# Where a kernel squares its input for the first RMS norm: transposed tiles in the first chunk, or a second, token-major load in the second chunk

## The chip, the cores and the metric

One core of one Trainium2 chip runs the kernel in one launch. The metric is the device time of the launch in microseconds (us); the kernel before takes 1688.6 us (median of three runs, 1688.39 to 1688.74). The five engines are named as in the profile: PE (TensorE, matmuls; PEld its weight loads), DVE (VectorE), ACT (ScalarE), POOL (GpSimd) and SP (SyncE, which here only issues transfers).

## The reference

One decoder layer for 256 tokens of width 4096, in float32: an RMS norm, one wide input projection, two attention mixers, a gate path, an output projection, a residual and a last RMS norm.

```python
h = _rmsnorm(x, norm_g[l])
proj = h @ w_in[l]
(q_a, k_a, v_a, z_a, q_b, kc, vc, ksl, vsl, kwn, vwn, z_b, g_b) = jnp.split(proj, ...)
o_a = _dilated_mixture(q_a, k_a, v_a, ...)      # dilated sliding-window attention, 16 heads
o_b = _nsa(q_b, kc, vc, ksl, vsl, kwn, vwn, ...)  # compressed, selected and window branch, 16 heads
y_a = _rmsnorm(o_a, out_g_a[l]) * silu(z_a)
y_b = _rmsnorm(o_b, out_g_b[l]) * silu(z_b)
x = x + concat(y_a, y_b) @ w_out[l]
return _rmsnorm(x, final_g)
```

The norm is `x * rsqrt(mean(x * x) + 1e-6) * g`. Its factor per token can be applied after the projection, since it is the same for all features of a token. So the sum of squares of a token isn't needed before the first product is scaled.

## The kernel before

**Tiles.** All wide products run as one stream of *chunks* of up to 512 output columns. A chunk sums over 32 *k-tiles* of 128 features, for two halves of 128 tokens. Its weights arrive in *units* of four k-tiles (1 MB) into three stage buffers. Every float32 operand is split in two float32r halves, `h` (a copy on ACT, line 102, or 105 with a scale) and `l` (the rest, on DVE, line 103 or 106), and each product is three matmuls (`mm3`, lines 95 to 97). So one k-tile costs six matmuls of 512 columns and a chunk 192. A unit is split in two half-units of two k-tiles (`split_unit`); the split runs two half-units ahead of the matmuls, in three buffers. For the first eight units, the ones of the first chunk, `split_x` also splits the k-tiles of `x`, scaled with `norm_g`, out of a transposed copy of `x` that `load_x` brings in eight pieces of 0.5 MB (SP's queue). Those pieces live in four buffers, tag `o`.

**The squares.** After the second half of each of the first eight units, `square_x` squares the piece of `x` on ACT (line 163) and POOL adds it to the squares before (line 165). When the first chunk has ended, `done_kvc` calls `token_rms`: two DVE adds (lines 176 and 177), four PE records that sum over partitions (line 180), and `rsqrt_mean` (DVE, then POOL's power, line 112). Only then ACT evicts the first chunk's two accumulators, scaled (line 513), to a tile of the tag `qk`, which has two buffers. There are four accumulators, so the third chunk needs those of the first.

**Background work.** What mixers and gates need is queued as tasks in a first-in, first-out queue. `run_stream` takes one step of it every second k-tile. The first chunk holds keys and values that are to be compressed: two `compress` tasks of 14 steps each, with their own weights (4 MB each, in the buffers of tag `o`). Chunks two to four are queries, keys and values of mixer A's first head group, whose task is queued at the end of the fourth. `hooks` calls a function at a given chunk and k-tile.

**Order.** The framework that builds the kernel orders each engine's instructions by the order of writing and by its own estimate of times, so neighbours can change places. Every engine and each transfer queue then works strictly in its order.

**The two ends.** The kernel begins with thirteen matmuls on zeros and one activation, written ahead of all loads (lines 121 to 127), to have PE and ACT's table ready. Then `run_stream` asks for three units of `x` (SP's queue) and weights (the first unit on ACT's queue, four transfers of one k-tile each, line 216). At the end the last chunk is multiplied for the first 128 tokens and then, from splits kept on chip, for the second 128; `finish` scales the residual rows of one half in eight pieces of 512 columns, in turn on DVE (line 846) and ACT (line 844), and stores each piece (line 847).

Of the kernel before, what the change touches and what calls it, by code (L numbers as in the profile page):

```python
# [11 lines left out]
F32 = mybir.dt.float32  # L12
# [33 lines left out]
# The three dilated patterns of mixer A share their scores and their ALiBi distances, so their  # L46
# softmaxes merged by their denominators are one softmax in which a key counts once for each
# pattern that holds it (MULT). With SEQ = 256 there are 4 selection blocks and SLC_TOP = 16, so
# the selected branch of mixer B holds every causal key, and its window of 512 does too.
# The columns of mixer B's scores are [window keys, later half first | compressed | selected keys].  # L50
# [28 lines left out]
def hybrid_trunk(ctx: ExitStack, tc: tile.TileContext, a: dict):  # L79
# [19 lines left out]
    def split_to(h, l, src, scale=None):  # L99
        """h + l = src * scale, both in float32r."""  # L100
        if scale is None:
            nc.scalar.activation(h, src, AF.Copy)  # L102
            nc.vector.tensor_sub(l, src, h.bitcast(F32))  # L103
        else:
            nc.scalar.activation(h, src, AF.Copy, scale=scale)  # L105
            nc.vector.scalar_tensor_tensor(l, src, scale, h.bitcast(F32), op0=OP.mult, op1=OP.subtract)  # L106

    def rsqrt_mean(out, ss, width):
        """out = (ss / width + eps) ** -0.5, for [P, n] sums of squares."""
        t = work.tile(list(out.shape), F32, name="rsq")  # L110
        nc.vector.tensor_scalar(t, ss, 1.0 / width, EPS, op0=OP.mult, op1=OP.add)
        nc.gpsimd.tensor_tensor(out, t, nhalf[:, : out.shape[1]], op=OP.pow)

# [6 lines left out]
    # while the first loads run: the tensor engine to its full clock, ScalarE's table  # L120
    idle = work.tile([P, CW], BF16, name="idle", tag="zt", bufs=4)
    nc.vector.memset(idle, 0.0)
    warm = psm.tile([P, CW], F32, name="warm", tag="ps")
    for _ in range(WARM):
        nc.tensor.matmul(warm, idle[:, :P], idle, start=True, stop=True)
    first = work.tile([P, 1], F32, name="first", bufs=1)
    nc.scalar.activation(first, ones, AF.Exp)

# [10 lines left out]
    squares = []  # L139

    x_raw = {}

    def load_x(piece):
        q, half = divmod(piece, 2)
        if half == 0:
            xh.append(big.tile([P, QK, SEQ], F32R, name=f"xh{q}", tag="x", bufs=8))
            xl.append(big.tile([P, QK, SEQ], F32R, name=f"xl{q}", tag="x", bufs=8))
        t = x_raw[piece] = big.tile([P, G4, SEQ], F32, name="xp", tag="o", bufs=4)
        step = 1 if piece == 0 else 2 if piece == 1 else G4
        for j in range(0, G4, step):  # L150
            nc.sync.dma_start(t[:, j : j + step], a["xT"][piece, :, j : j + step])
            if piece == 0 and j == 0:
                nc.sync.dma_start(g_in, a["norm_g"])

    def split_x(k):
        """One k-tile of x, times norm_g, split."""
        (q, i), (piece, j) = divmod(k, QK), divmod(k, G4)
        split_to(xh[q][:, i], xl[q][:, i], x_raw[piece][:, j], g_in[:, k : k + 1])

    def square_x(piece):  # L160
        """The squares of four k-tiles of x, added to those before."""
        sq = work.tile([P, G4, SEQ], F32, name="sq", tag="qk", bufs=2)
        nc.scalar.activation(sq, x_raw.pop(piece), AF.Square)  # L163
        if squares:
            nc.gpsimd.tensor_tensor(squares[0], squares[0], sq, op=OP.add)  # L165
        else:
            squares.append(sq)

    # 1 / rms of the tokens, and what the projections are scaled by
# [4 lines left out]
    def token_rms():  # L174
        sq = squares[0]
        nc.vector.tensor_add(sq[:, 0:2], sq[:, 0:2], sq[:, 2:4])
        nc.vector.tensor_add(sq[:, 0], sq[:, 0], sq[:, 1])
        s = psm.tile([P, NT], F32, name="ss", tag="ps")
        for m in range(NT):
            nc.tensor.matmul(s[:, m : m + 1], sq[:, 0, m * P : (m + 1) * P], ones, start=True, stop=True)  # L180
        rsqrt_mean(rstd, s, DM)
        nc.vector.tensor_scalar_mul(nrstd, rstd, -1.0)
        nc.vector.tensor_scalar_mul(rstd_q, rstd, SCALE)

# [14 lines left out]
    # A unit is one load: k-tiles k0 ... of one chunk of output columns, used in two halves.  # L199
# [11 lines left out]
    def stage_unit(u):  # L211
        src, width, k0, n, c = units[u]
        t = stage.tile([P, n, width], F32, name="w", tag="w")
        if u == 0:
            for j in range(n):
                nc.scalar.dma_start(t[:, j : j + 1], src[:, j : j + 1])
        elif u < 4:
            for j in range(0, n, 2):
                nc.sync.dma_start(t[:, j : j + 2], src[:, j : j + 2])
        else:  # L220
            nc.sync.dma_start(t, src)
        staged[u] = t

    def split_unit(u, half):
        t = staged[u]
        src, width, k0, n, c = units[u]
        n //= 2
        h = split.tile([P, n, width], F32R, name="wh", tag="wh")
        l = split.tile([P, n, width], F32R, name="wl", tag="wl")
        w = 1 if u == 0 else n  # L230
        for j in range(0, n, w):
            if u < 8:
                for k in range(k0 + half * n + j, k0 + half * n + j + w):
                    split_x(k)
            split_to(h[:, j : j + w], l[:, j : j + w], t[:, half * n + j : half * n + j + w])
        if half == 1 and u < 8:
            square_x(u)
        splitted[u, half] = (h, l)
# [4 lines left out]
    def split_held(u, half, i):  # L243
        """One eighth of the last chunk, split and kept on chip."""
# [15 lines left out]
    hooks = {}  # (chunk, k-tile): work that becomes possible there  # L260

    def run_stream():
# [4 lines left out]
        for i, (u, s) in enumerate(subs):  # L267
            while True:
                if n_st < len(units) and n_st <= u + (2 if i else 0):
                    if n_st < 8:  # L270
                        load_x(n_st)
                    stage_unit(n_st)
                    n_st += 1
                    if n_st == 6:
                        late_loads()
# [40 lines left out]
        # the last chunk again, for the second half of the tokens  # L316
# [25 lines left out]
    def evict_split(key):  # L342
        def done(ps):
            # [tokens, head, (h, l), d]: the two halves of a head side by side
# [7 lines left out]
    def transposed(src, key, tag):  # L352
        """[tokens, 4 heads * d] -> float32r halves of [d, 4 heads, tokens]."""
# [28 lines left out]
    def pipeline(units, stages, at):  # L382
        """Stage i of a unit is done at[i] steps of the background work after its first."""
# [7 lines left out]
    def attend_a(hg):  # L391
# [34 lines left out]
        def values(j):  # L426
            ph, pl, rden = live.pop(j)
            head = hg * 4 + j
            # columns: with h and with l of the values
# [55 lines left out]
    def turn_y(which, f0):  # L485
        """Features f0 * 128 ... of y (two heads), turned and split for the output projection."""
# [19 lines left out]
    # rows 0 ...: h, rows 32 ...: l, rows 64 ...: h of the compressed values, zeros between  # L506
# [10 lines left out]
    def compress(t, which):  # L517
        """gelu((blocks + pe) @ w1) @ w2 of the keys (0) or the values (1), both groups."""
# [63 lines left out]
        # gelu in its tanh form  # L582
# [39 lines left out]
    # keys and values of the two other branches: selected (0) and window (1)  # L622
# [56 lines left out]
    def attend_half(hg, m):  # L679
        """Four heads of mixer B that share their keys, one half of the tokens."""  # L680
# [52 lines left out]
        # (columns of n, halves of the values)  # L733
# [5 lines left out]
        def turn(i):  # L739
# [10 lines left out]
            if vl is None:  # L750
                # rows that meet h, l and h of the values: h, h and l
# [78 lines left out]
    def finish(m, gf):  # L830
# [4 lines left out]
        for i in range(8):  # L835
# [11 lines left out]
            nc.sync.dma_start(a["out"][m * P : (m + 1) * P, i * CW : (i + 1) * CW], t)  # L847

# [10 lines left out]
    add_chunk(w_chunk(20), CW, x_lhs, done_kvc)  # L859
# [13 lines left out]
    # y of mixer A and the first half of mixer B are turned as the last chunk frees x  # L873
# [17 lines left out]
def _tiles(w, n):  # L891
    """[4096, n * 512] -> [n, 8, 128, 4, 512]: contiguous blocks of four k-tiles."""
# [41 lines left out]
```

## Time and profile before

| What | Value |
|---|---|
| time, median of three runs | 1688.6 us (1688.39 to 1688.74) |
| profiled execution | span 1686.2 us from the first to the last instruction; its time outside the span is not given |
| PE busy | 1667.2 us (99%), 8071 matmuls |
| DVE busy | 1023.2 us (61%) |
| ACT busy | 814.7 us (48%) |
| POOL busy | 24.3 us (1%), 16 instructions |
| transfers | 319.97 MB, mean 190 GB/s over the span |
| mean granted clock of PE | 0.998 |

A row of the timeline has the start, the duration, the engine and line, the operation with the tile it writes and the tiles it reads, the number of merged instructions and, in brackets, the idle time before them with what ended it. A row of the windows table has a stretch, its length, the busy time and the number of instructions of each engine, the granted clock, the share of the transfer engines and their GB/s. A row of waits has who waited for whom, the total, the number of waits and the longest one. A row of the chain has the start, the duration and what the end of the run depended on at that time. A row of a group has its line, engine and form, the count, busy time and mean duration in ns, and the idle time ahead of it. "L96" is line 96 of the kernel; a helper's line stands for all who call it. Matmuls overlap, so a matmul's 0.39 us is longer than the distance to the next one.

### The profile page before, as it was taken

How to read it: one execution, taken by the hardware profiler on the slowest of the kernel's cores; microseconds unless marked ns; L12 is line 12 of the kernel's file. 1: busy time of each engine (PE TensorE's matmuls, PEld its weight loads, DVE VectorE, ACT ScalarE, POOL GpSimd, SP SyncE). 2: the span in 40 equal slices, each digit the busy share in tenths (PEclk: the TensorE clock that was granted, in tenths of full speed). 3: DMA queues.
4: the chain of work that ended last, by engine and by line, in shares of the span. 5: the costliest groups of instructions: out<-in, count | busy, mean ns of one | idle time of the engine just before them, and what ended most of it. 6: DMA issues, size and time to landing. Idle time of an engine off the chain costs nothing.

```text
span 1686.2 us, 20334 instructions
## 1 busy us (share of the span) xinstructions
PE 1667.2 (99%) x8071; PEld 1394.2 (83%) x8071; DVE 1023.2 (61%) x1389; ACT 814.7 (48%) x1121; POOL 24.3 (1%) x16
## 2 busy tenths in 40 slices
PE   8999999999999999999999999999999999999997
PEld 5788888888888888998888888888888888888887
DVE  8865474465456447456858678576667855555553
ACT  7654454445445445445545455454445544444443
POOL 3100000000000000000000000000000000000000
PEclk9999999999999999999999999999999999999999
DMA  8764545544554554465354444645555456655654
GB/s 321 281 250 150 199 150 191 187 171 175 199 181 169 187 190 166 139 225 186 135 190 150 175 166 146 213 151 187 193 185 196 167 202 218 213 205 212 209 199 160
DMA packets 51791, 319.97 MB, mean 190 GB/s; under 512 B 6128, under 2 KB 7664, under 8 KB 15856
## 3 DMA queue, kind: packets, MB, share of 16 engines
q1 hardware_dynamic: 47376, 311.33, 51.4%
q10 hardware_dynamic: 4320, 7.34, 1.3%
q8 instruction: 63, 1.03, 0.3%
q14 instruction: 32, 0.26, 0.0%
HBM read 314.46 MB, written 4.19 MB: 189 GB/s over the span
## 4 chain that ended last, share of the span: by engine, by line
PE 95%; DVE 2%; issue 1%; ACT 1%; DMA 1%; SPq 0%; ACTq 0%; POOLq 0%; POOL 0%; DVEq 0%
PE acc L96 29%; PE acc L95 29%; PE acc L97 29%; DVE xl L106 1%; PE pt L747 1%; DVE wl L103 1%; PE pt L361 1%; PE s L96 1%; PE s L95 1%; PE s L97 1%; ACT wh L102 0%; PE ph L572 0%; PE ph L573 0%; PE pt L496 0%; DMA w<-in_w_in 0%
## 5 line engine op out<-in xcount | busy, mean ns | idle before, releaser
L103 DVE TENSOR_TENSOR wl<-w,wh 128x1024 fp32r<-128x1024 f32 (+2 forms) x562 | 677.7, 1206 | 582.3 <-ACT wh L102 579.1
L102 ACT ACTIVATE wh<-w 128x1024 fp32r<-128x1024 f32 (+2 forms) x562 | 588.2, 1047 | 722.8 <-PE acc L97 678.4
L96 PE MATMUL acc<-wl,xh 128*128 128x512 f32 (+2 forms) x1792 | 688.0, 384 | 5.6 <-DVE wl L103 5.6
L95 PE MATMUL acc<-wh,xh 128*128 128x512 f32 (+2 forms) x1792 | 690.6, 386 | 1.6 <-ACT wh L102 1.6
L97 PE MATMUL acc<-wh,xl 128*128 128x512 f32 (+2 forms) x1792 | 686.9, 383 | 0.0
L96 PEld LDWEIGHTS acc<-wl,xh 128*128 128x128 f32 x1792 | 337.1, 188 | 71.0 <-DVE wl L103 10.0
L97 PEld LDWEIGHTS acc<-wh,xl 128*128 128x128 f32 x1792 | 336.8, 188 | 65.9
L95 PEld LDWEIGHTS acc<-wh,xh 128*128 128x128 f32 x1792 | 336.8, 188 | 64.3 <-ACT wh L102 2.5
L95 PE MATMUL acc<-wh,yh 128*128 128x512 f32 (+1 forms) x512 | 192.9, 377 | 0.0
L97 PE MATMUL acc<-wh,yl 128*128 128x512 f32 (+1 forms) x512 | 192.5, 376 | 0.0
L96 PE MATMUL acc<-wl,yh 128*128 128x512 f32 (+1 forms) x512 | 192.4, 376 | 0.0
L97 PEld LDWEIGHTS acc<-wh,yl 128*128 128x128 f32 x512 | 96.4, 188 | 17.7
L96 PEld LDWEIGHTS acc<-wl,yh 128*128 128x128 f32 x512 | 96.4, 188 | 17.5
L95 PEld LDWEIGHTS acc<-wh,yh 128*128 128x128 f32 x512 | 96.4, 188 | 17.2
L477 DVE RECIPROCAL ez<-ez 128x512 f32<-128x512 f32 x16 | 53.6, 3349 | 0.2
L704 ACT ACTIVATE nb<-nb,mn 128x128 f32<-128x128 f32 (+1 forms) x64 | 28.7, 449 | 25.8 <-DVE mn L702 24.7
L106 DVE SCALAR_TENSOR_TENSOR xl<-xp,g_in,xh 128x256 fp32r<-128x256 f32 x32 | 29.0, 943 | 5.6 <-ACT xh L105 5.6
L412 ACT ACTIVATE n<-n,mn 128x128 f32<-128x128 f32 (+1 forms) x32 | 13.4, 456 | 24.5 <-DVE mn L410 24.5
L697 DVE SCALAR_TENSOR_TENSOR nb<-cmat,s 128x272 f32<-128x272 f32 (+1 forms) x48 | 19.6, 428 | 5.9 <-PE s L97 5.7
L165 POOL TENSOR_TENSOR sq<-sq 128x1024 f32<-128x1024 f32 x7 | 20.9, 2984 | 30.5 <-ACT sq L163 30.5
L105 ACT ACTIVATE yh<-pt,g_out 128x256 fp32r<-128x256 f32 x32 | 14.5, 464 | 12.9 <-DVE yl L106 12.9
L821 DVE TENSOR_TENSOR r<-acc,xr 128x512 f32<-128x512 f32 (+1 forms) x18 | 10.6, 625 | 15.5 <-PE acc L97 15.5
(236 smaller groups left out, 957.0 us busy)
## 6 DMA issues: line engine op xcount, KB each, us to landing
w<-in_w_in SPq DMA_DIRECT2D x204, 1024.0 KB, 4.8
w<-in_w_out SPq DMA_DIRECT2D x64, 1024.0 KB, 4.8
w<-in_w_vg SPq DMA_DIRECT2D x8, 608.0 KB, 3.8
w<-in_cmp_k_w SPq DMA_DIRECT2D x4, 1024.0 KB, 8.2
w<-in_cmp_v_w SPq DMA_DIRECT2D x4, 1024.0 KB, 7.8
w<-in_w_kw SPq DMA_DIRECT2D x4, 1024.0 KB, 4.8
out<-r SPq DMA_DIRECT2D x16, 256.0 KB, 2.8
xr<-in_x ACTq DMA_DIRECT2D x7, 512.0 KB, 5.2
```

Source lines behind the costliest of these rows:

```text
L95: nc.tensor.matmul(out, lh, rh, start=start, stop=False)
L96: nc.tensor.matmul(out, lh, rl, start=False, stop=False)
L97: nc.tensor.matmul(out, ll, rh, start=False, stop=stop)
L102: nc.scalar.activation(h, src, AF.Copy)
L103: nc.vector.tensor_sub(l, src, h.bitcast(F32))
L106: nc.vector.scalar_tensor_tensor(l, src, scale, h.bitcast(F32), op0=OP.mult, op1=OP.subtract)
L165: nc.gpsimd.tensor_tensor(squares[0], squares[0], sq, op=OP.add)
L361: nc.tensor.transpose(pt[:, j, m], src[:, m, hh * HD : (hh + 1) * HD], ident)
L477: nc.vector.reciprocal(e, e)
L697: nc.vector.scalar_tensor_tensor(n[:, j, a0:a1], DB[m][:, a0 - lo : a1 - lo], SLOPES[hg * 4 + j], s, op0=OP.mult, op1=OP.subtract)
L704: nc.scalar.activation(n[:, j, sec], n[:, j, sec], AF.Exp, bias=mn[:, i : i + 1], scale=-1.0, accum_out=den[:, i : i + 1])
L747: nc.tensor.transpose(pt[:rows, j], src, ident)
```

## The change

The transposed pieces of `x` are no longer squared. Eight tiles of `x` in token-major order (128 tokens by 1024 features each, 0.5 MB) are loaded again, in the buffers of tag `o`, on SP's queue behind the weights of units 8 to 15, which are those of the second chunk. After the second half of each of these units ACT squares one tile in place and accumulates the sum along the row, so that no sum over partitions is left for PE and none for POOL. `token_rms` is one DVE reduction and the same `rsqrt_mean`. The eviction of the first chunk, with the queueing of the two `compress` tasks, moves from the end of the first chunk to k-tile 29 of the second. At the start, `norm_g` is loaded ahead of the first piece of `x`; the first unit's `x` and weights come in three transfers each (one, one and two k-tiles) in place of four; the warm-up is written behind the first unit's loads. At the end two scaled pieces are stored together, after the second one.

```diff
-    for _ in range(WARM):
-        nc.tensor.matmul(warm, idle[:, :P], idle, start=True, stop=True)
-    nc.scalar.activation(first, ones, AF.Exp)
...
     def load_x(piece):
...
-        step = 1 if piece == 0 else 2 if piece == 1 else G4
-        for j in range(0, G4, step):
-            nc.sync.dma_start(t[:, j : j + step], a["xT"][piece, :, j : j + step])
-            if piece == 0 and j == 0:
-                nc.sync.dma_start(g_in, a["norm_g"])
+        if piece == 0:
+            nc.sync.dma_start(g_in, a["norm_g"])
+            for j, e in ((0, 1), (1, 2), (2, 4)):
+                nc.sync.dma_start(t[:, j:e], a["xT"][piece, :, j:e])
+        elif piece == 1:
+            for j in range(0, G4, 2):
+                nc.sync.dma_start(t[:, j : j + 2], a["xT"][piece, :, j : j + 2])
+        else:
+            nc.sync.dma_start(t, a["xT"][piece])
...
-    def square_x(piece):
-        sq = work.tile([P, G4, SEQ], F32, name="sq", tag="qk", bufs=2)
-        nc.scalar.activation(sq, x_raw.pop(piece), AF.Square)
-        if squares:
-            nc.gpsimd.tensor_tensor(squares[0], squares[0], sq, op=OP.add)
-        else:
-            squares.append(sq)
+    x_nat = {}
+    ssx = cst.tile([P, NT, 4], F32, name="ssx")
+
+    def load_x_nat(i):
+        m, q = divmod(i, 4)
+        t = x_nat[i] = big.tile([P, DM // 4], F32, name="xn", tag="o", bufs=4)
+        nc.sync.dma_start(t, a["x"][m * P : (m + 1) * P, q * DM // 4 : (q + 1) * DM // 4])
+
+    def square_x(i):
+        m, q = divmod(i, 4)
+        t = x_nat.pop(i)
+        nc.scalar.activation(t, t, AF.Square, accum_out=ssx[:, m, q : q + 1])
...
     def token_rms():
-        sq = squares[0]
-        nc.vector.tensor_add(sq[:, 0:2], sq[:, 0:2], sq[:, 2:4])
-        nc.vector.tensor_add(sq[:, 0], sq[:, 0], sq[:, 1])
-        s = psm.tile([P, NT], F32, name="ss", tag="ps")
-        for m in range(NT):
-            nc.tensor.matmul(s[:, m : m + 1], sq[:, 0, m * P : (m + 1) * P], ones, start=True, stop=True)
+        s = work.tile([P, NT], F32, name="ss")
+        nc.vector.reduce_sum(s, ssx, axis=AX.X)
         rsqrt_mean(rstd, s, DM)
...
         if u == 0:
-            for j in range(n):
-                nc.scalar.dma_start(t[:, j : j + 1], src[:, j : j + 1])
+            for j, e in ((0, 1), (1, 2), (2, 4)):
+                nc.scalar.dma_start(t[:, j:e], src[:, j:e])
...
-        if half == 1 and u < 8:
-            square_x(u)
+        if half == 1 and 8 <= u < 16:
+            square_x(u - 8)
...
+    def warm_up():
+        idle = work.tile([P, CW], BF16, name="idle", tag="zt", bufs=4)
+        nc.vector.memset(idle, 0.0)
+        warm = psm.tile([P, CW], F32, name="warm", tag="ps")
+        for _ in range(WARM):
+            nc.tensor.matmul(warm, idle[:, :P], idle, start=True, stop=True)
+        first = work.tile([P, 1], F32, name="first", bufs=1)
+        nc.scalar.activation(first, ones, AF.Exp)
...
                     stage_unit(n_st)
+                    if 8 <= n_st < 16:
+                        load_x_nat(n_st - 8)
                     n_st += 1
+                    if n_st == 1:
+                        warm_up()
...
-            nc.sync.dma_start(a["out"][m * P : (m + 1) * P, i * CW : (i + 1) * CW], t)
+            if i % 2:
+                nc.sync.dma_start(a["out"][m * P : (m + 1) * P, (i - 1) * CW : (i + 1) * CW],
+                                  res[q, m][:, at - CW : at + CW])
...
-    add_chunk(w_chunk(20), CW, x_lhs, done_kvc)
+    first_ps = []
+    add_chunk(w_chunk(20), CW, x_lhs, first_ps.extend)
+    hooks[1, 29] = lambda: done_kvc(first_ps)
```

More of the change, by code (lines that the diff above doesn't have):

```diff
@@ L119, in hybrid_trunk @@
     nc.vector.memset(ones, 1.0)
-    idle = work.tile([P, CW], BF16, name="idle", tag="zt", bufs=4)
-    nc.vector.memset(idle, 0.0)
-    warm = psm.tile([P, CW], F32, name="warm", tag="ps")
-    for _ in range(WARM):
-        nc.tensor.matmul(warm, idle[:, :P], idle, start=True, stop=True)
-    first = work.tile([P, 1], F32, name="first", bufs=1)
-    nc.scalar.activation(first, ones, AF.Exp)
     cmat = cst.tile([P, N_CONST], F32, name="cmat")
@@ L137, in hybrid_trunk @@
     xh, xl = [], []
-    squares = []
     x_raw = {}
```

## The prediction

> **What bounds the kernel now.** I read the page first (TensorE, PE in the profile, is busy 99% of the span), then the windows table over three stretches, then the waits of PE over the whole program, to find where the rest of PE's time is.
>
> ```profile
> core 0: us, PE busy (x) PEld busy (x) DVE busy (x) ACT busy (x) POOL busy (x), PEclk, DMA share, GB/s
> 7.14:60.56 53.42, 47.03 (x195) 35.38 (x195) 49.36 (x53) 37.94 (x58) 20.89 (x7) 1.00 0.76 288
> 60.90:104.40 43.50, 43.40 (x223) 35.75 (x223) 30.33 (x30) 26.31 (x30) 0.71 (x1) 1.00 0.72 271
> ...
> 61.00:1664.00 1603.00, 1602.74 (x7764) 1344.95 (x7764) 966.90 (x1314) 768.12 (x1047) 2.11 (x3) 1.00 0.52 186
> ```
> ```profile
> PE acc L96 <- DVE wl L103: 5.6, 8, 1.1
> PE acc L95 <- ACT wh L102: 1.6, 2, 0.8
> ```
>
> From 61 to 1664 us PE is idle for 0.26 us. So nothing between the second chunk and the last one can be won except by removing matmuls, and the change removes none there. All of PE's waits for splits of weights lie in the first 60 us: the first chunk, its 192 matmuls starting at 7.14 and ending where the sum-of-squares matmuls begin, at 60.56. How long would it take unhindered? Two rows of the timeline, six matmuls apart, give the pace:
>
> ```profile
> 52.43 0.39 PE L95 MATMUL acc<-wh,xh 128*128 128x512 f32 x1
> ...
> 53.79 0.39 PE L95 MATMUL acc<-wh,xh 128*128 128x512 f32 x1
> ```
>
> 1.36 us for six is 0.2267 us each, so 192 take 43.5 us. The first chunk takes 53.42: **9.9 us of PE time are lost in it**. The chain of waits, cut to that chunk, says to what:
>
> ```profile
> 1.65 4.83 DMA xp<-in_xT
> 6.50 6.59 DMA w<-in_w_in
> 13.11 1.06 ACT wh L102
> ...
> 43.53 3.73 DVE xl L106 x4
> 49.53 2.33 DVE xl L106
> ...
> 60.56 0.34 PE ss L180 x4
> ```
>
> First loads until 13 us, then ScalarE (ACT), which has squares between its splits, then VectorE (DVE) until 55 us. DVE is long because single splits of x are stretched: the first and the last of seven such places, and the same instruction later in the run with nothing on GpSimd (POOL):
>
> ```profile
> 16.95 2.66 POOL L165 TENSOR_TENSOR sq<-sq 128x1024 f32<-128x1024 f32 x1 [16.51 <-ACT sq L163]
> 17.30 2.99 DVE L106 SCALAR_TENSOR_TENSOR xl<-xp,g_in,xh 128x256 fp32r<-128x256 f32 x2
> ...
> 48.57 3.21 POOL L165 TENSOR_TENSOR sq<-sq 128x1024 f32<-128x1024 f32 x1 [2.79 <-ACT sq L163]
> 49.45 3.80 DVE L106 SCALAR_TENSOR_TENSOR xl<-xp,g_in,xh 128x256 fp32r<-128x256 f32 x4
> 53.18 0.68 DVE L176 TENSOR_TENSOR sq<-sq 128x512 f32<-128x512 f32 x1
> ...
> L106 DVE SCALAR_TENSOR_TENSOR xl<-xp,g_in,xh 128x256 fp32r<-128x256 f32 x32 | 29.0, 943 | 5.6 <-ACT xh L105 5.6
> ...
> L106 DVE SCALAR_TENSOR_TENSOR yl<-pt,g_out,yh x32: 473/477/486, 1289.3 to 1352.1; 128x256 fp32r<-128x256 f32 x32
> ```
>
> 32 splits of x should take 32 x 0.477 = 15.3 us and take 29.0: 13.7 us of DVE time, about 2 us for each of POOL's seven sums of squares.
>
> **Squares out of the first chunk.** Gone from it: eight squares on ACT, seven sums on POOL, two DVE adds (0.68 and, at half the size, some 0.4 us), and four PE records, 0.34 us. Per unit of four k-tiles DVE then needs 4 x 0.477 + 2 x 1.21 = 4.3 us, ACT 4 x 0.49 + 2 x 1.05 = 4.1 us, and PE 24 x 0.2267 = 5.4 us. PE becomes the bound of the chunk, with over 1 us to spare per unit, provided that the loads come. A unit brings 1.5 MB, so 5.4 us want about 290 GB/s; the table has 288 over the whole stretch, and the transfers of the first 60 us in slices of 1.5 us say what is there when it is asked for:
>
> ```profile
> GB/s 0 115 188 356 386 339 153 322 423 418 421 412 415 410 431 418 320 131 344 409 436 383 399 399 268 104 306 306 0 87 306 306 0 71 333 306 0 0 202 431
> ```
>
> Over 400 from 12 to 24 us, and zeros later, when all stage buffers are full. I take it that loads keep up after the opening.
>
> **The opening.** Rows of the timeline:
>
> ```profile
> 1.17 1.28 ACT L127 ACT_TABLE_LOAD   x1 [1.17 <-PEq L923]
> 1.18 0.42 SPq L153 DMA_DIRECT2D g_in<-in_norm_g  x1
> 1.25 5.05 PE L125 MATMUL warm<-idle 128*128 128x512 bf16 x13 [1.25 <-DVE idle L122]
> 5.19 0.82 ACTq L216 DMA_DIRECT2D w<-in_w_in  x2
> 6.06 0.51 ACT L105 ACTIVATE xh<-xp,g_in 128x256 fp32r<-128x256 f32 x1 [3.39 <-DMA g_in<-in_norm_g]
> ...
> 7.14 0.73 PE L95 MATMUL acc<-wh,xh 128*128 128x512 f32 x2 [0.84 <-ACT wh L102]
> ...
> 14.22 0.73 PE L95 MATMUL acc<-wh,xh 128*128 128x512 f32 x2 [0.78 <-ACT wh L102]
> ...
> 15.48 0.50 PE L96 MATMUL acc<-wl,xh 128*128 128x512 f32 x1 [0.53 <-DVE wl L103]
> ...
> DMA to landing us min/median/max: 4.3/4.7/4.8
> ```
>
> The last row is for the first pieces of x. The third and fourth pieces of the first weights were issued only at 5.19, when earlier transfers had landed, and ACT, which issues them, could start its first split only when it was done with that, at 6.01. In the new order norm_g goes first (0.74 instead of 1.18) and x second (1.18); x then lands at 1.18 + 4.4 = 5.6 and the first split starts there if ACT has no issue left to do, since there are three weight pieces instead of four. The first matmul came 1.08 us after the first split; 5.65 + 1.08 = 6.7: **0.4 us earlier** (bounds: 0.6 later, if the third piece on ACT still waits until 5.2, to 0.6 earlier).
>
> What idle is left in the chunk? The first wait for a low half (about 0.3 us) stays. The second unit: its weights landed at 13.09 and PE went on at 14.22 and 15.48. With one issue less on each queue the first weight load of the second unit can go out up to 1 us sooner, and the pieces ahead of it are no longer held until 5.2; I take 11.5 for its landing. Then 1.05 (high half) and a DVE turn behind it let PE go on near 13, where it would have finished the first unit at 6.7 + 5.4 + 0.3 = 12.4. That is 0.6 and, for the low half, 0.7 more. Together **1.6 us left of 9.9** (bounds 0.3, everything early, and 4.7, worked out under the rivals).
>
> **Squares in the second chunk.** Added: eight loads of 0.5 MB on SP's queue, each behind the weight load of its unit, and eight squares on ACT. One square of this size costs 1.05, and reading its accumulator 0.19:
>
> ```profile
> L163 ACT ACTIVATE sq<-xp 128x1024 f32<-128x1024 f32 x8 | 8.4, 1047 | 0.0
> ...
> L448 ACT ACTIVATION_READ_ACCUMULATOR junk<-o_a x8: 187/188/193, 262.3 to 682.6; 128x1 f32 x8
> ```
>
> 8 x 1.24 = 9.9 us of ACT in a stretch where it is busy 26.3 of 43.5, and the compression's splits of its own weights leave that stretch, since they start a chunk later. The 4 MB take the place of 4 MB of compression weights, with which PE lost 0.1 us there. Both are hidden by PE; without that cover they would cost 9.9. A square waits in ACT's queue ahead of the next weight splits, so a late load would hold them and PE; the load is issued right behind weights that arrive well ahead of their use, so I cost it at nothing.
>
> **The later eviction.** The chain that now follows the first chunk:
>
> ```profile
> 60.94 0.16 DVE L111 TENSOR_SCALAR rsq<-ss 128x2 f32<-128x2 f32 x1 [0.75 <-PE ss L180]
> 61.18 0.71 POOL L112 TENSOR_TENSOR rstd<-rsq,nhalf 128x2 f32<-128x2 f32 x1 [9.39 <-DVE rsq L111]
> 61.92 1.27 ACT L513 ACTIVATE kvc<-acc,rstd 128x512 f32<-128x512 f32 x2 [0.27 <-POOL rstd L112]
> ```
>
> From 60.94 to 63.19 it is 2.25 us, plus a small reduction in place of the adds. It starts two k-tiles, 2.7 us, before the third chunk wants the first chunk's accumulators back. PE waits at most for this chain if it comes late (2.4), else not at all; queued behind it on ACT are the next high halves, which have one to two half-units of lead. The compression's 28 steps, two a unit, then run through the third chunk and into the fourth and end before mixer A's first task, which is queued at the end of the fourth. I take **0.3 us later** (0 to 2.4).
>
> **The last stores.** Four of 512 KB in place of eight of 256 KB for the last 128 tokens:
>
> ```profile
> 1677.99 1.95 ACT L844 ACTIVATE r<-r,rout 128x512 f32<-128x512 f32 x3 [1.05 <-POOL rout L112]
> 1677.99 1.68 DVE L846 TENSOR_SCALAR r<-r,rout 128x512 f32<-128x512 f32 x4 [0.67 <-POOL rout L112]
> 1678.51 0.81 SPq L847 DMA_DIRECT2D out<-r  x2
> GB/s 0 0 0 0 0 0 0 0 0 213 377 401 361 401 385 385 393 352 401 385 344 393 393 369 393 393 377 393 377 385 377 140 0 0 0 0 0 0 0 0
> ```
>
> The last row is the window 1677 to 1687 in quarter microseconds: data flows from about 1679.35 to 1685.0, 2.1 MB at some 375 GB/s, so the engines of the DMA, not the issue, set the end. A pair is ready only with its ACT half, 1677.99 + 0.65 = 1678.64 instead of 1678.42: the flow starts 0.15 to 0.2 later. If rows of 4 KB go at 420 it takes 5.0 instead of 5.6 and ends 0.4 sooner; at 375 it ends 0.2 later. I take **0.2 earlier**. The Trainium skill (DMA: Bandwidth & Descriptors, Anatomy of one DMA) gives a transfer a constant part of about 2.0 us plus bytes at 436 GB/s; by that the last store alone would land an estimated 0.6 us later after its issue. The trace has 256 KB landing in 2.0 to 3.0 us, so the constant part is there; with it the end would still be the flow's.
>
> **The sum.** 0.4 (start) + 8.3 (9.9 - 1.6) + 0.34 (four PE records) - 0.3 + 0.2 = 8.9 us earlier. The profiled span is 1686.2, so 1677.3; its own time around the span isn't given, and the median of the timed runs, 1688.6, lies 2.4 above the span. With the same 2.4: **1679.7 us**.
>
> **The rivals.** *The opening stays bound by loads* (0.20). The second unit comes at 14.22 and 15.48 as now: 0.3 + (14.22 - 12.4 = 1.8) + 0.8, and 0.3 for each of the other six units make 4.7 idle: 1682.8. For it: the chain has DMA until 13.1, and merging pieces doesn't lessen the bytes. Against: the later pieces are held by earlier landings, which merging relieves.
>
> *The eviction stops PE* (0.07): 2.4 us instead of 0.3, 1681.8. Against it: the squares it needs are over before the hook.
>
> *The warm-up comes late* (0.06). It is now written after the first issues. If the table load (1.28) and the first activation (0.20) stand behind a third weight issue at 5.19, the first split starts at 7.0 in place of 5.65: 1681.1. If instead PE's warm-up starts late, the first real matmuls run slow. The thirteen warm-up matmuls took 5.05 us, 0.39 each, against 0.2267 later. The Trainium skill (TensorE: Matmul & The Clock Gate, Part 1: The HAM clock gate) says that the array runs at half clock until it has been busy for about 3.4 us; by that, an estimate of 1.7 us would be lost. The trace agrees in kind, though its clock column says 1.00 throughout.
>
> *POOL isn't what stretches DVE* (0.03). Then DVE keeps its 13.7 us and the chunk gains only the two adds (1.1), the PE records, the start and the stores, less 0.3: 1.7 us, 1686.9, no change that can be told. Against it: in both quoted places the stretched split ends with POOL's sum.
>
> *The second load of x chokes the second chunk* (0.04), the case on the other side. It needs 8.4 + 4.2 = 12.6 MB. PE hides this in 43.5 us at 290 GB/s; the gain is gone when it takes 52.4, at 240 GB/s. At 200 it takes 63, 19.5 more than 43.5, and the time is 1679.7 + 19.5 = 1699. Against it: 271 GB/s went there with PE full, and slices of the first chunk reach over 400.
>
> **How the numbers follow.** The forecast itself has 0.60. It and the first three rivals (0.93) all lie faster by more than 0.2%, 3.4 us, which is about what a measurement of this kernel can tell from no change; the fourth lies within (0.03), the fifth above (0.04). The low end is the forecast with 0.3 idle left, nothing for the eviction and 0.4 for the stores, with a little for the start: 1677.6. The high end takes in the load-bound opening and the two other small rivals: 1683.2.
>
> **What would show it.** Right: no POOL work of size before the second chunk, all splits of x near 0.48 us, the first chunk's matmuls over in 45 us from a start near 6.7, PE full in the second and third chunk, stores ending at most 0.4 us closer to the last scaling. Wrong: PE idle behind weight loads after 15 us (first rival), PE waiting for kvc (second), ACT idle for the token-major x with PE idle behind it (fifth), or splits of x still stretched (fourth).

## The result and the profile after

The changed kernel takes **1678.83 us** (median of four runs, 1678.58 to 1679.02), the kernel before 1688.67 beside it (1688.39 to 1689.3). The ratio is 0.994, 95% interval 0.9926 to 0.9954: 9.8 us faster, forecast 8.9. The profiled span went from 1686.2 to 1676.9, by 9.3 us.

The windows table of the changed kernel, over the two first chunks and over a stretch of 1603 us behind them, as long as the one shown of before (columns: stretch, length, busy time and instructions of each engine, granted clock, share and GB/s of the transfers):

```profile
core 0: us, PE busy (x) PEld busy (x) DVE busy (x) ACT busy (x) POOL busy (x), PEclk, DMA share, GB/s
7.42:51.60 44.18, 43.96 (x191) 35.54 (x192) 33.77 (x51) 31.64 (x52) 0.00 (x0) 1.00 0.95 377
51.60:95.50 43.90, 43.90 (x197) 36.35 (x196) 22.65 (x24) 27.68 (x35) 0.70 (x1) 1.00 0.76 282
52.00:1655.00 1603.00, 1602.85 (x7767) 1345.65 (x7767) 967.06 (x1315) 775.76 (x1061) 2.10 (x3) 1.00 0.53 188
```

The first chunk had 53.42 us and PE busy for 47.03 of it; now its 192 matmuls are over in some 44.2. In the second chunk PE is busy without a gap, with the eight squares added. The later 1603 us are as full as they were. So the whole gain is made before 52 us.

The groups of DVE in the first chunk, and all of PE's waits in the whole program:

```profile
L103 DVE TENSOR_TENSOR wl<-w,wh 128x1024 fp32r<-128x1024 f32 x16 | 19.6, 1224 | 9.8 <-ACT wh L102 9.7
L106 DVE SCALAR_TENSOR_TENSOR xl<-xp,g_in,xh 128x256 fp32r<-128x256 f32 x32 | 13.9, 479 | 5.8 <-ACT xh L105 5.8
```
```profile
PE acc L95 <- ACT wh L102: 1.6, 1, 1.6
PE warm L262 <- DVE idle L259: 1.2, 1, 1.2
PE acc L96 <- DVE wl L103: 0.2, 1, 0.2
```

The 32 splits of x kept DVE busy for 29.0 us before and for 13.9 now, at a mean of 479 ns in place of 943 (overlaps of neighbours count once in the busy time). DVE's splits of whole half-units of weights now wait 9.7 us for ACT; before, where DVE was the bound, they waited 2.0. PE waits for a low half once, for 0.2 us, instead of eight times for 5.6 us; the 1.6 us are its wait ahead of the first matmul.

The timeline of the opening:

```profile
0.74 1.37 ACTq L210 DMA_DIRECT2D w<-in_w_in  x3
6.34 0.51 ACT L105 ACTIVATE xh<-xp,g_in 128x256 fp32r<-128x256 f32 x1 [2.70 <-DMA xp<-in_xT]
7.42 0.73 PE L95 MATMUL acc<-wh,xh 128*128 128x512 f32 x2 [1.60 <-ACT wh L102]
...
8.13 0.51 ACT L105 ACTIVATE xh<-xp,g_in 128x256 fp32r<-128x256 f32 x1 [0.76 <-DMA xp<-in_xT]
...
9.94 0.50 PE L96 MATMUL acc<-wl,xh 128*128 128x512 f32 x1 [0.22 <-DVE wl L103]
...
11.71 1.05 ACT L102 ACTIVATE wh<-w 128x1024 fp32r<-128x1024 f32 x1
```

The three first weight transfers go out without the hold until 5.19. The first matmul comes no earlier than before (7.42 against 7.14), but behind 9.94 PE never waits in this chunk, and the second unit's first split (11.71) waits for no load, where it began at 13.11.

The eviction and the end:

```profile
81.36 0.18 ACT L165 ACTIVATION_READ_ACCUMULATOR xn<-xn 128x1 f32 x1
82.17 1.06 ACT L102 ACTIVATE wh<-w 128x1024 fp32r<-128x1024 f32 x1 [0.62 <-PE acc L97]
83.14 1.25 ACT L521 ACTIVATE kvc<-acc,rstd 128x512 f32<-128x512 f32 x2
```
```profile
GB/s 0 0 0 0 0 0 0 0 0 0 0 0 115 377 410 377 426 393 410 426 377 442 377 426 393 410 393 393 393 426 442 377 442 164 0 0 0 0 0 0
...
out<-r SPq DMA_DIRECT2D x4, 512.0 KB, 3.7
```

The eviction is done at 84.4. The second chunk ends 2 x 43.5 + 0.7 us behind 7.42, at about 95.1, so that is some 11 us ahead of the third chunk: the chain stands close behind the last square (one split of weights lies between), not where the hook is written, at k-tile 29, near 91 us. The second fence is the window 1667 to 1677 in quarter microseconds and the last four stores, with the time from issue to landing. The last stores flow from about 1670.1 to 1675.3. From the last scaling (1668.64) to the end of the span it is 8.26 us; it was 8.21.

### The profile page after: what moved, and what is told of

The parts are those of the page before. It is cut to its first block, busy times and chain, and to the rows that moved or that the text cites. A ratio compares the mean times of both kernels' runs of the same rounds, so it can differ in the third digit from the quotient of the medians.

```text
span 1676.9 us, 20307 instructions
## 1 busy us (share of the span) xinstructions
PE 1663.4 (99%) x8067; PEld 1394.5 (83%) x8067; DVE 1008.0 (60%) x1388; ACT 815.6 (49%) x1129; POOL 3.4 (0%) x9
## 4 chain that ended last, share of the span: by engine, by line
PE 98%; issue 1%; DMA 0%; ACT 0%; DVE 0%; SPq 0%; ACTq 0%; POOLq 0%; POOL 0%
PE acc L95 30%; PE acc L96 30%; PE acc L97 30%; PE pt L755 1%; PE pt L369 1%; PE s L97 1%; PE s L96 1%; PE s L95 1%; PE ph L581 0%; PE ph L580 0%; PE pt L504 0%; DMA xp<-in_xT 0%; PE po L443 0%; PE po L444 0%; PE po L97 0%
## 5 line engine op out<-in xcount | busy, mean ns | idle before, releaser
L710 DVE TENSOR_REDUCE mn<-nb 128x1 f32<-128x128 f32 (+1 forms) x64 | 19.5, 345 | 0.6
L447 ACT ACTIVATE o_a<-po,rden 128x128 f32<-128x128 f32 x32 | 11.5, 359 | 16.2 <-DVE o_a L448 16.2
```

Of the source, the lines that this page charges most:

```text
L710: nc.vector.tensor_reduce(mn[:, i : i + 1], n[:, j, sec], axis=AX.X, op=OP.min)
```

## The experiments

The theory: POOL's seven sums make DVE's splits last longer, DVE sets the pace of the first chunk, and that is most of the 9.9 us that PE loses there. The rivals: ACT's squares did it; the order of the loads did it; POOL's work costs its time wherever it stands.

**The parts alone.** The stores alone, put into the kernel before:

```diff
-            nc.sync.dma_start(a["out"][m * P : (m + 1) * P, i * CW : (i + 1) * CW], t)
+            if i % 2:
+                nc.sync.dma_start(..., res[q, m][:, at - CW : at + CW])
```

> The kernel before with the paired last stores alone. The trace after shows 8.26 us from the last scaling to the end of the span where the one before has 8.21, but the time outside the span is 1.8 us where it was 2.4 by the median. If the stores do nothing at all, the time is 1688.6. If the 0.5 us outside the span belong to them, it is 1688.1.

Measured: 1689.12 us, ratio 1.0005 (0.9996 to 1.0014). No difference that can be told.

The opening alone (the hunks of `load_x`, of the first unit in `stage_unit`, and `warm_up`):

```diff
+            nc.sync.dma_start(g_in, a["norm_g"])
+            for j, e in ((0, 1), (1, 2), (2, 4)):
+                nc.sync.dma_start(t[:, j:e], a["xT"][piece, :, j:e])
...
+            for j, e in ((0, 1), (1, 2), (2, 4)):
+                nc.scalar.dma_start(t[:, j:e], src[:, j:e])
```

> The kernel before with the new opening alone (norm_g first, first unit in three transfers each, warm-up written behind them); squares, sums, eviction and stores as before. My theory (POOL's sums stretch DVE's splits, and DVE bounds the first chunk): DVE and ACT still set the pace after 15 us, so at most 1 us is won, 1687.7 to 1689.0, and seven splits of x still last over 2 us. Rival (the loads of the opening held the chunk back): 1680 to 1682.

Measured: 1687.91 us, ratio 0.9995 (0.9986 to 1.0004). Its splits of x and PE's waits (groups and waits of this run, first 60 and 70 us) are those of before:

```profile
L106 DVE SCALAR_TENSOR_TENSOR xl<-xp,g_in,xh 128x256 fp32r<-128x256 f32 x32 | 29.0, 946 | 6.2 <-ACT xh L105 6.2
```
```profile
PE acc L96 <- DVE wl L103: 5.7, 9, 1.1
```

The squares in the second chunk with the later eviction, alone:

```diff
-        if half == 1 and u < 8:
-            square_x(u)
+        if half == 1 and 8 <= u < 16:
+            square_x(u - 8)
...
+    hooks[1, 29] = lambda: done_kvc(first_ps)
```

> The kernel before with the squares from a token-major load in the second chunk and the later eviction; opening and stores as before. My theory: the first matmul stays at 7.1, the second unit still comes at 14.2 and 15.5, and from there PE never waits, so that the first chunk ends at 15.5 + 166 x 0.2267 = 53.1 in place of 60.9: 1680.9. Rival (the opening held the chunk back): 1688.

Measured: 1682.23 us (1680.64 to 1683.15), ratio 0.9961 (0.9948 to 0.9975): 6.4 us of the 9.8, and 1.3 us above the 1680.9 that I expected. The profiled execution is the one of 1680.64. The opening's stops are still in its timeline:

```profile
10.29 0.63 ACT L102 ACTIVATE wh<-w 128x512 fp32r<-128x512 f32 x1 [1.69 <-DMA w<-in_w_in]
...
14.77 0.51 PE L95 MATMUL acc<-wh,xh 128*128 128x512 f32 x1 [0.28 <-ACT wh L102]
...
16.03 0.50 PE L96 MATMUL acc<-wl,xh 128*128 128x512 f32 x1 [0.75 <-DVE wl L103]
```

So the parts don't add up: by the medians the opening is worth 0.8 us while DVE bounds the chunk (an interval that includes nothing at all), and 1682.23 - 1678.83 = 3.4 us once it doesn't (the stores, in both differences' reach, showed nothing). The rows above come from an execution that is only 1.9 us behind the changed kernel's profiled one (1680.64 against 1678.70).

PE's clock is probably a part of the rest. Three of the four other executions of this run have a mean granted clock of 0.997 in place of 0.998. None of them was profiled, but one with 0.996 and the same old opening was: that of the run below with neither squares nor sums, 1684.99 us where its other three took 1681.01 to 1681.32. PE there waits 2.5 us for the second unit, until 14.80, and then starts its matmuls 0.43 us apart instead of 0.23 until about 20.7. Two windows of that execution:

```profile
16.00:20.00 4.00, 4.00 (x13) 3.19 (x13) 4.00 (x8) 4.00 (x9) 0.00 (x0) 0.50 1.00 380
21.00:25.00 4.00, 4.00 (x19) 3.25 (x19) 3.60 (x7) 3.00 (x6) 0.00 (x0) 1.00 0.98 347
```

The granted clock is 0.50 in the first and 1.00 in the second. It fell 1.7 us into the wait, at about 14.0. The profiled execution of the stores alone (1691.2 us, median 1689.12) has the same: a wait of 2.6 us and a clock of 0.50 from 16 to 20. That the wait makes the clock fall was not tested.

**Which part of the squares?** POOL's sums left out, ACT's squares kept:

```diff
-        if squares:
-            nc.gpsimd.tensor_tensor(squares[0], squares[0], sq, op=OP.add)
-        else:
+        if not squares:
             squares.append(sq)
```

> The kernel before without POOL's seven sums: ACT still squares all eight pieces in the first chunk, but only the squares of the first piece enter the norm. So the sums over the other seven pieces are left out. My theory (POOL stretches DVE): the splits of x last 0.48 us each, ACT needs 4.1 + 1.05 = 5.15 us for a unit, still under PE's 5.44, and most of the gain is there: 1681 to 1683. Rival (the squares in ACT's queue hold the weight splits): 1687 or more.

Measured: 1680.79 us (1680.51 to 1683.11), ratio 0.9955 (0.9943 to 0.9968), 0.2 below what I expected. ACT's squares left out, POOL at work:

```diff
-        nc.scalar.activation(sq, x_raw.pop(piece), AF.Square)
...
+        x = x_raw.pop(piece)
+        if piece == 1:
+            squares.append(work.tile([P, G4, SEQ], F32, name="sq", tag="qk", bufs=2))
+            nc.gpsimd.tensor_tensor(squares[0], x, x, op=OP.mult)
+        elif piece > 1:
+            nc.gpsimd.tensor_tensor(squares[0], x, x, op=OP.mult)
```

> The kernel before without ACT's eight squares; POOL still does seven operations of the same size, now products of the raw pieces with themselves, of which the last one stands in for the sum. So the squares are not summed over the pieces. My theory (POOL alone holds DVE): hardly faster than before, 1686 to 1689, splits of x over 2 us in seven places. Rival (ACT's squares cost too): 1684 or less.

Measured: 1686.17 us (1684.8 to 1687.78), ratio 0.9983 (0.9974 to 0.9992), the low end of what I expected. And neither of the two:

```diff
+        if piece == 0:
...
+            nc.scalar.activation(squares[0], x, AF.Square)
```

> The kernel before with one square of the first piece alone and no sums on POOL. So the squares of seven pieces are left out. It is the run without POOL's sums (1680.8) less seven squares on ACT. My theory: PE was already the bound there but for the opening, so at most 0.8 us more is won: 1680 to 1681. Rival (ACT's squares hold PE up by themselves, about 1 us for each): 1675 or less.

Measured: 1681.16 us (1681.01 to 1684.99), ratio 0.9956 (0.9943 to 0.997), 0.2 above what I expected. With the kernel before these are four corners:

| | POOL's seven operations | none |
|---|---|---|
| ACT's eight squares | 1688.7 | 1680.8 |
| at most one square | 1686.2 | 1681.2 |

POOL costs 7.9 us beside the squares and 5.0 without them. Without POOL the squares cost nothing, so the rival that gave the loss to ACT is out. With POOL the two corners are 2.5 apart, but not by the squares alone: the seven products start when a raw piece has landed and take 18.0 us together, while the seven sums wait for ACT's squares and take 20.9. What the squares cost beside POOL stays open. The splits of x and of whole half-units of weights in the first chunk, in this order: without POOL, with POOL alone, with neither, from the execution of 1684.99 us (groups of DVE, 7 to 60 us; the number behind the bar is the busy time, then the mean in ns):

```profile
L103 DVE TENSOR_TENSOR wl<-w,wh 128x1024 fp32r<-128x1024 f32 x18 | 22.0, 1224 | 10.7 <-ACT wh L102 10.6
L106 DVE SCALAR_TENSOR_TENSOR xl<-xp,g_in,xh 128x256 fp32r<-128x256 f32 x32 | 14.0, 480 | 5.0 <-ACT xh L105 5.0
```
```profile
L103 DVE TENSOR_TENSOR wl<-w,wh 128x1024 fp32r<-128x1024 f32 x17 | 25.6, 1517 | 3.1 <-ACT wh L102 3.0
L106 DVE SCALAR_TENSOR_TENSOR xl<-xp,g_in,xh 128x256 fp32r<-128x256 f32 x32 | 18.8, 628 | 5.0 <-ACT xh L105 5.0
```
```profile
L103 DVE TENSOR_TENSOR wl<-w,wh 128x1024 fp32r<-128x1024 f32 x17 | 20.8, 1223 | 11.7 <-ACT wh L102 11.7
L106 DVE SCALAR_TENSOR_TENSOR xl<-xp,g_in,xh 128x256 fp32r<-128x256 f32 x32 | 13.9, 479 | 5.0 <-ACT xh L105 5.0
```

With POOL at work a mean split of weights goes from 1223 to 1517 ns and one of x from 479 to 628; the splits of weights wait 3.1 us for ACT instead of 10.7 and more. I had expected seven splits of x over 2 us in the run with POOL alone; there are three, and with them three splits of weights at 2.9 us. In the kernel before, no split of weights is stretched (the 16 of whole half-units take 1214 ns in the mean). There the first sum starts at 16.95, while a split of weights runs from 16.13 in its usual 1.22 us, and the split of x behind it, at 17.30, is held. In the run with POOL alone the product at 15.42 starts in a split of x, and the split of weights behind it, at 15.80, takes 2.92. So it isn't the splits of x as such that are stretched, but whichever split begins while POOL is at work. The Trainium skill (GPSIMD Engine Reference, 1. Specifications) states that POOL's SBUF interfaces are shared with VectorE, with contention for DVE instructions that have two SBUF inputs. Both kinds of split have two, and the traces agree.

**Where POOL's work stands.** The same kind of operation put into the changed kernel, in the second chunk:

```diff
         nc.scalar.activation(t, t, AF.Square, accum_out=ssx[:, m, q : q + 1])
+        nc.gpsimd.tensor_tensor(t, t, t, op=OP.add)
```

> The changed kernel with eight POOL operations of the same size put into the second chunk (each squared tile is added to itself; nothing reads it). My theory has two parts. The stretch is a matter of POOL and DVE at the same time: weight splits on DVE in the second chunk last up to 3 us or start later. And it costs only where DVE has no slack: DVE is busy 22.7 of 43.9 us there, eight times 2 us more leave it under PE's pace, so the time stays at 1678.8 within 0.5. Rival (POOL's work costs its 2 us each wherever it stands): 1690 or more.

Measured: 1678.68 us (1678.41 to 1679.68), ratio 0.9936 (0.9922 to 0.9949). POOL's 15 us there cost nothing, but one half of what I expected to see is not there (windows, POOL's group, and a row of DVE's timeline):

```profile
51.60:95.50 43.90, 43.90 (x197) 36.37 (x196) 25.02 (x23) 27.68 (x35) 15.29 (x9) 1.00 0.78 290
```
```profile
L166 POOL TENSOR_TENSOR xn<-xn 128x1024 f32<-128x1024 f32 x8 | 15.4, 1921 | 68.6 <-ACT xn L165 68.6
...
82.79 1.67 DVE L111 TENSOR_SCALAR rsq<-ss 128x2 f32<-128x2 f32 x1
```

DVE's busy time rose by 2.4 us only (22.65 to 25.02), with one instruction fewer in the window. The largest part, 1.5 us, is the one small instruction of the last row, which takes 0.17 us in the changed kernel and here began during POOL's last addition (82.54 to 84.43). The longest split of weights is 1.45 us, not up to 3: POOL started in the last 0.3 us of a split, was over when the next had hardly begun, and took 1.92 us with little in its way. In the kernel before the same size took 2.98 in the mean. The run shows that POOL's work is free where it meets DVE's idle time; it doesn't show how much stretching the second chunk would bear. The counterpart, in the first chunk:

```diff
+        if half == 1 and u < 8:
+            x = x_raw.pop(u)
+            nc.gpsimd.tensor_tensor(x, x, x, op=OP.add)
```

> The changed kernel with eight POOL operations put into the first chunk instead: each transposed piece of x is added to itself after its splits, and nothing reads it. It is the counterpart of the run with the same operation in the second chunk (1678.7). My theory (POOL beside DVE costs where DVE has little slack): 1682 to 1686, PE waiting for low halves again. Rival (POOL's work was not the cause, the squares' other parts were): 1678.8.

Measured: 1681.61 us (1681.37 to 1681.7), ratio 0.9955 (0.9943 to 0.9968): 2.8 us lost against the changed kernel, a little less than the low end of what I expected. The groups of DVE and the waits of PE:

```profile
L106 DVE SCALAR_TENSOR_TENSOR xl<-xp,g_in,xh 128x256 fp32r<-128x256 f32 x32 | 25.3, 833 | 5.9 <-ACT xh L105 5.9
```
```profile
PE acc L96 <- DVE wl L103: 1.7, 4, 1.2
PE acc L95 <- ACT wh L102: 1.5, 2, 1.3
```

DVE takes 11.4 us more for the splits of x (25.3 against 13.9), and PE feels a quarter of it. The rest goes into the slack that DVE had.

**The opening's pieces.** First x ahead of norm_g again:

```diff
-            nc.sync.dma_start(g_in, a["norm_g"])
             for j, e in ((0, 1), (1, 2), (2, 4)):
                 nc.sync.dma_start(t[:, j:e], a["xT"][piece, :, j:e])
+                if j == 0:
+                    nc.sync.dma_start(g_in, a["norm_g"])
```

> The changed kernel with the first piece of x issued ahead of norm_g again. The first split waits for x, which landed 5.1 us after its issue at 1.18; issued at 0.74 it should land 0.4 us sooner, and the first matmul should start near 7.0 instead of 7.42: 1678.4. If norm_g, issued second, is then late in its place, nothing changes: 1678.8.

Measured: 1678.74 us (1678.52 to 1679.4), ratio 0.9937 (0.9925 to 0.995). The first matmul does start earlier, if only by 0.3 us, since the first split now waits for norm_g, until 6.06. Then the next pieces of x hold the splits (timeline):

```profile
7.14 0.73 PE L95 MATMUL acc<-wh,xh 128*128 128x512 f32 x2 [1.44 <-ACT wh L102]
...
7.47 0.51 ACT L105 ACTIVATE xh<-xp,g_in 128x256 fp32r<-128x256 f32 x1 [0.39 <-DMA xp<-in_xT]
...
8.82 0.51 ACT L105 ACTIVATE xh<-xp,g_in 128x256 fp32r<-128x256 f32 x1 [0.32 <-DMA xp<-in_xT]
```

The first unit's weights in four transfers again:

```diff
-            for j, e in ((0, 1), (1, 2), (2, 4)):
-                nc.scalar.dma_start(t[:, j:e], src[:, j:e])
+            for j in range(n):
+                nc.scalar.dma_start(t[:, j : j + 1], src[:, j : j + 1])
```

> The changed kernel with the first unit's weights in four transfers again, all else of the new opening kept. My theory: a transfer more on each side brings the late issue back, so that ACT issues the fourth piece only when an earlier one has landed (about 5 us) and waits for it in its queue; PE loses 1 to 3 us in the first unit: 1680 to 1682. Rival (the number of pieces is nothing, the order of the issues is): 1678.8.

Measured: 1679.68 us (1679.31 to 1680.51), ratio 0.9945 (0.9933 to 0.9958): 0.85 us lost. The row of the four issues and the split that waited for the last piece:

```profile
0.73 4.53 ACTq L210 DMA_DIRECT2D w<-in_w_in  x4
...
11.38 0.63 ACT L102 ACTIVATE wh<-w 128x512 fp32r<-128x512 f32 x1 [1.04 <-DMA w<-in_w_in]
```

The four issues last until 5.26 where three were out at 2.11, and the last piece is late by 1 us. The size is just below the 1 to 3 us that I expected. The warm-up written first again (its seven lines moved back ahead of the loads):

```diff
+    for _ in range(WARM):
+        nc.tensor.matmul(warm, idle[:, :P], idle, start=True, stop=True)
...
+    nc.scalar.activation(first, ones, AF.Exp)
     cmat = cst.tile([P, N_CONST], F32, name="cmat")
```

> The changed kernel with the warm-up written ahead of all loads again. My theory: the table load and the first activation only change places with a weight issue on ACT, and all of it is over by 4 us, before x lands: 1678.8 within 0.4. Rival (the table load ahead of the third weight issue makes the first unit late): 1680 or more.

Measured: 1678.77 us (1678.69 to 1678.94), ratio 0.9939 (0.9925 to 0.9953): no difference. And the sixteen single stores in the changed kernel:

```diff
-            if i % 2:
-                nc.sync.dma_start(..., res[q, m][:, at - CW : at + CW])
+            nc.sync.dma_start(a["out"][m * P : (m + 1) * P, i * CW : (i + 1) * CW], t)
```

> The changed kernel with sixteen single stores again. My theory: the transfers' rate sets the end either way, so 1678.8 within 0.4. If the 0.5 us that the changed kernel has less outside its span come from the four transfers fewer at the end, 1679.3.

Measured: 1678.76 us (1678.63 to 1678.92), ratio 0.9939 (0.9926 to 0.9951). None of these four versions beats the changed kernel by more than 0.1 us, and the pairs of stores are worth nothing in either kernel.

Of the opening's 3.4 us the transfers of the weights give 0.85. The order of norm_g and the warm-up give nothing. What the three transfers of x in place of four give wasn't run by itself, and the run with the old opening spreads over 2.5 us, in part with PE's clock. Against the two runs without POOL's work, which also have the old opening (1680.79 and 1681.16), the changed kernel gains 2.0 and 2.3 us, with the squares' other parts included. So 3.4 is more likely too much than too little, and how the rest beyond 0.85 divides stays open.

## Why the prediction was right

*What bounds the kernel.* Right: the time came out of the first chunk, where 9.9 us were lost, and the stretched splits were the main cause, with 7.9 us for POOL's sums alone. The rival that POOL isn't to blame fell with the run without the sums. One step of the reading was too narrow: I gave the stretching to the splits of x; the run with POOL alone shows weight splits stretched as well. And its 13.7 us of stretching set a sum of durations (15.3) against a busy time (29.0); busy time against busy time it is 29.0 - 13.9 = 15.1.

*The start*, 0.4 us earlier: it isn't there. The first matmul came at 7.42, 0.28 later. The failed step is that x lands 4.4 us after its issue: ACT, idle until then, began its split at 6.34, 5.2 us after the issue at 1.18. (4.4 is what norm_g took from that place in the kernel before.) The stated bound, 0.6 later, held.

*Idle left in the chunk*, 1.6 us: measured about 0.7. Eight matmuls lie ahead of 9.94, 2.52 us after the first one, where 8 x 0.2267 = 1.81 would do; behind that none. I had the second unit wait for its weights; they were there. Start and idle together: 6.7 + 1.6 = 8.3 forecast, 7.42 + 0.7 = 8.1 measured. Two errors of 0.7 and 0.9 us cancel, which is luck as far as the runs show; that both come from more bytes being on their way early is argued, not shown. The absent wait also is the answer to the first rival: with the old opening its stops are there (14.77 and 16.03 in the run of the squares alone), with the new one not.

*The late warm-up*, a rival: it didn't come, and the order in which it is written makes no difference (1678.77). But first matmuls at half pace do occur. In the profiled execution with POOL in the second chunk the warm-up was over at 5.8, the first matmul came at 7.69, and the granted clock was 0.50 from 8 to 11 us; it took 1679.68 where the other four took 1678.41 to 1678.68.

*Squares in the second chunk*, nothing: right. PE is busy 43.90 of 43.90 us with 282 GB/s of transfers, against the 290 that I asked for to hide it and the 240 below which the rival of the choked chunk would have won.

*The eviction*, 0.3 later: nothing measured. The step that failed is that the chain starts at the hook. It was over some 11 us before its end was needed. *The last stores*, 0.2 earlier: 0.05 later in the span and nothing in two timed pairs. They flow faster (the full slices have 405 GB/s in the mean, 383 before; the 375 of the prediction was a little low) and start later, as worked out. By the slices, each read to about 0.1 us, the flow is 0.3 us shorter, starts 0.2 later after the last scaling, and the span ends 0.2 later after the flow. A transfer of 512 KB landed 3.7 us after its issue in the median, one of 256 KB 2.8 in the kernel before. The Trainium skill (DMA: Bandwidth & Descriptors, Anatomy of one DMA) has a larger transfer land later by its bytes, in a fit for transfers that GpSimd issues; by its figure that is an estimated 0.6 us here. The trace agrees in direction. I had set that aside; that it took the gain is not shown.

*The sum*: 9.3 us of span against 8.9. The timed gain, 9.84, is 0.5 more, because I carried 2.4 us outside the span over from a single profiled execution. In the 45 executions of the kernel before that were timed beside the experiments, the time outside the span is 1.83 to 1.95 us, and in the 34 of the changed kernel and its variants 1.74 to 1.84. So the change does next to nothing there, some 0.1 us. The 2.4 set the span of one execution (1686.2) against the median time of others, whose spans have a median of 1686.8. The four executions of the changed kernel have 1677.05; that difference, 9.75, and the 0.1 are the timed gain. So the forecast was 0.9 us too small and not 0.4.

## What to carry to other kernels

Work on GpSimd isn't free because GpSimd is idle: set beside a VectorE that bounds its stage, seven operations of 128 x 1024 cost 5.0 and 7.9 us; in the changed kernel's first chunk, where VectorE has some slack, eight cost 2.8, and in its second chunk, where VectorE is idle half the time, nothing. Read a group's mean duration against the same instruction elsewhere in the run (943 against 477 ns here) before putting a stage down to its engine's amount of work. And parts of a change that share a stage aren't to be added up: the new order of the loads was worth 0.8 us, if anything, behind one bound and 2 to 3.4 without it.

## What the runs showed of the hardware that I had not expected

POOL's own time depends on DVE: the same addition of 128 x 1024 took 1.92 us in the mean in the second chunk and 3.13 (2.27 to 3.89) beside the splits in the first; the kernel before's sums took 2.98 there. A DVE instruction that is already running isn't stretched; the one that begins while POOL is at work is, in one place even one of two columns (0.17 to 1.67 us).

Fewer, larger first transfers didn't start the first matmul sooner but ended the opening's stops, and the times lie closer together: eleven executions of the opening alone within 0.43 us (1687.68 to 1688.11), 21 of the kernel before beside them within 3.3 (1687.69 to 1690.98). With the old opening PE's granted clock fell to 0.50 for some 6 us in two profiled executions, behind waits of 2.5 and 2.6 us in the first 15 us.
